# Two recurrences of a layer on TensorE: matmuls of both directions side by side in array halves, outputs ordered by form

## The chip, the cores and the metric

One Trainium2 chip, one of its cores. The metric is the device time of one execution in microseconds: the median of the runs shown. A core has TensorE (PE in the profile, its weight loads PEld), VectorE (DVE), ScalarE (ACT), GpSimd (POOL) and SyncE (SP), which issues most DMAs here. PE writes its products to PSUM, eight banks of 128 partitions by 2 KB.

## The reference, cut to what matters

A layer has 512 latent tokens and 256 context tokens of width 1024. Two mixers run beside each other, each with 8 heads of 128 channels, each in both directions over chunks of 64 tokens: 4 context chunks, then 8 latent chunks. Each head and direction carries a state `S` of 128 by 128 from chunk to chunk.

```
def step(S, xs):                                    # branch A, gated DeltaNet
    u_c, w_c, qd_c, kd_c, qk_c, tot_c = xs
    v_new = u_c - jnp.einsum('bhcd,bhdv->bhcv', w_c, S)
    o_c = jnp.einsum('bhcd,bhdv->bhcv', qd_c, S) + jnp.einsum('bhij,bhjv->bhiv', qk_c, v_new)
    S = tot_c[..., None, None] * S + jnp.einsum('bhcd,bhcv->bhdv', kd_c, v_new)
    return S, o_c
...
def step(S, xs):                                    # branch B, HGRN2
    qd_c, kd_c, v_c, tot_c = xs
    o_c = jnp.einsum('bhcd,bhdv->bhcv', qd_c, S)
    S = tot_c[..., :, None] * S + jnp.einsum('bhcd,bhcv->bhdv', kd_c, v_c)
    return S, o_c
```

The outputs of both directions are added, normed and gated. The branches are merged, and an expert layer of 16384 experts follows, which takes about the second half of the time and is not touched here.

## The kernel before, in words

The program is a list of Python generators whose steps are interleaved in proportions (`weave`, `mixed`). From that list the framework that builds the program places each engine's instructions in a fixed order before the run; an instruction may be placed ahead of others that come earlier in the list but aren't ready by the framework's reckoning. It also sets all waits. Two accesses of one PSUM tile that lie in the same bank are put in order, whatever parts of the bank they touch, unless both are on the same engine.

PSUM is split in three pools: three banks `a` (`bank`), two banks `s` (`quad`, four blocks of 128 columns) and three banks `pj` for projections.

*Branch A* (lines 469 to 759). For each head `h`, `scan(h)` runs beside `prepare(h + 1)` (keys, queries, values by projection, the inverse of a triangular matrix in `levels`), beside `ada_rows`, and beside `fill`, projections that later stages need. A projection (`proj`) is a run of matmuls of 512 or 256 columns in three parts (lines 99 to 101) over weights split by ScalarE (line 94) and VectorE (line 95).

`scan(h)` has 12 steps, 4 over context and 8 over latents. In step `i` the first direction is at chunk `i`, the second at the last but `i`, so that the two always lie in different halves of the 128 partitions (`blk` gives block, half and half's number; `slot` gives the place of a step's pair in the tiles `TB`, `vn` and `edS`, in which the upper half is stored in reverse). One step:

- for each direction, the product of keys and state (line 714, "KS") into its half of block 0 of a `quad`, then a VectorE step on 64 partitions that adds the values (line 715, tile `tmp`); in the first step ScalarE copies the values instead (line 712);
- one matmul with the inverse `TB` for both directions (line 717) into block 1;
- VectorE scales it to `vd` (line 720), and over latents ScalarE copies it to `vn` (line 722);
- for each direction, the product of keys and `vd` (line 726, "K") into block 2 or 3, then a VectorE step that makes the new state (line 732 or 734).

A step takes a `quad` of its own. After the last, the outputs of both directions are made in one `quad` (lines 742 to 747): for each chunk and direction `qd` by state (line 745), then `qk` by `vn` (line 746). `finish` norms and gates them, with another `quad`.

*Branch B* (lines 763 to 913). For each head, `scan_b(h)` runs beside `prepare_b(h + 1)` and `fill`. It has 11 steps; in each, for each direction, one matmul (line 883, K again) into a quarter of a `quad`, which two steps share, then a copy or a VectorE step that makes the new state (line 892). The outputs (lines 899 and 903) use a `bank`.

KS and line 745 use 128 rows by 64 columns of the array, line 746 uses 64 by 64, lines 726 and 883 use 64 by 128, `TB` and the projections all of it. The profile writes these forms as `128*64` and so on.

Of the kernel before, what the change touches and what calls it, by code (L numbers as in the profile page):

```python
# [9 lines left out]
F32 = mybir.dt.float32  # L10
# [50 lines left out]
def program(nc, tc, A, out, dbg=None):  # L61
# [14 lines left out]
    def bc(ap, n):  # L76
        """[p, a] -> [p, a, n]"""
        return ap[:, :, None].to_broadcast([ap.shape[0], ap.shape[1], n])

    def bm(ap, n):  # L80
        """[p, a] -> [p, n, a]"""
        return ap[:, None, :].to_broadcast([ap.shape[0], n, ap.shape[1]])
# [137 lines left out]
    def proj(g, ctx):  # L220
        """128 channels on partitions: [128, 512 latents], [128, 256 context]"""
# [10 lines left out]
    def mixed(*gens):  # L232
        """the steps of several generators in turn, in proportion to the numbers given; a third item marks
        one that need not end here"""
        g = [[x[0], 0, x[1], True, len(x) > 2] for x in gens]
        while any(x[3] and not x[4] for x in g):
            x = min((x for x in g if x[3]), key=lambda x: (x[1] + 1) / x[2])
            x[1] += 1
            x[3] = next(x[0], x) is not x
            yield  # L240
# [69 lines left out]
    def nat(ap):  # L310
        """scan-ordered latents read in natural order"""
        return ap.rearrange("p (c r) -> p r c", r=8)

# [8 lines left out]
    def turned(t, p, steps, b0, n, x):  # L322
        """the upper half of the partitions with directions and blocks in reverse: [p, d, b, x]"""
# [5 lines left out]
    def slot(i, ctx):  # L329
        """a step's place: the chunks of both directions lie in different halves of the partitions"""  # L330
# [108 lines left out]
    def ada_rows():  # L439
        """the rest of the adaLN projection as rows: g1, shift 2, scale 2, g2"""  # L440
# [28 lines left out]
    with tc.tile_pool(name="pA", bufs=1) as pA:  # L469
        # natural order with a zero before, between and after latents and context  # L470
# [10 lines left out]
        def diag(t, z):  # L481
            """the block of a half of the partitions"""
# [7 lines left out]
        def head(t, h):  # L490
            """[p, b, (d h)] -> [p, d, b] of a head"""
# [5 lines left out]
        def conv(dst, ci, ctx):  # L497
# [15 lines left out]
            S.activation(dst, cv[:, :w], AF.Silu)  # L513
# [24 lines left out]
        def prepare(h):  # L538
# [4 lines left out]
            # decays of both directions  # L543
# [11 lines left out]
            # gram matrices, [chunk row, chunk column]  # L555
# [7 lines left out]
            V.scalar_tensor_tensor(br[:, 2], head(eg, h), -1.0, rnk, op0=OP.mult, op1=OP.mult)  # L563
            qk = pA.tile([128, 2, 4, 64], F32, name="qk", bufs=2)
            G.tensor_tensor(qk, E_[:, :, :4], m_in2[:, :, None, :].to_broadcast([128, 2, 4, 64]), op=OP.mult)
            # minus the strict part's entries (the masks come later)
            G.tensor_tensor(E_, E_, br[:, 1, :, :, None].to_broadcast([128, 2, 6, 64]), op=OP.mult)
            V.tensor_tensor(E_, E_, gl_[:, None].to_broadcast([128, 2, 6, 64]), op=OP.mult)
            # diagonal blocks of 16 inverted with a block on each partition
# [49 lines left out]
            yield from conv(vT, 16 + h, True)  # L619
# [10 lines left out]
            H[h] = (kt, qn, rnq, br, qk, ktm, vtm, GA[h])  # L630
            yield

        def ahead(h):
            """the gate of a head and the keys of the next"""
# [54 lines left out]
        def scan(h):  # L689
            kt, qn, rnq, br, qk, ktm, vtm, ga = H[h]  # L690
# [7 lines left out]
            prev = [None, None]  # L698
            for st in range(12):
# [4 lines left out]
                q4 = quad()  # L704
                tmp = pA.tile([128, 128], F32, name="tmp", bufs=3)
                C = []
                for d in range(2):
# [3 lines left out]
                    if prev[d] is None:  # L711
                        S.copy(tmp[s], vtm[s, b])
                    else:
                        T.matmul(q4[s, 0], ksl(kt, c, ctx), prev[d], start=True, stop=True)
                        V.scalar_tensor_tensor(tmp[s], q4[s, 0], br[s, 2, d, b:b + 1], vtm[s, b],
                                               op0=OP.mult, op1=OP.add)
                T.matmul(q4[:, 1], TB[:, sd, sb], tmp, start=True, stop=True)
                if more:
                    vd = pA.tile([128, 128], F32, name="vd", bufs=3)
                    V.tensor_scalar(vd, q4[:, 1], edS[:, sd, sb, h:h + 1], None, op0=OP.mult)  # L720
                if not ctx:
                    S.copy(vn[:, sd, sb], q4[:, 1])
                for d, (b, s, hf) in enumerate(C):
                    lt = order[d][1]
                    if more:
                        T.matmul(q4[:, 2 + d], ktm[s, b], vd[s], start=True, stop=True)
                        if ctx and i < 3:
                            nxt = pA.tile([128, 128], F32, name="sc_", bufs=3)
                        else:
                            nxt = Sx[d][:, lt[0] if ctx else lt[i + 1]]  # L730
                        if prev[d] is None:
                            V.tensor_copy(nxt, q4[:, 2 + d])
                        else:
                            V.scalar_tensor_tensor(nxt, prev[d], etot[:, hf, b, 8 * d + h:8 * d + h + 1],
                                                   q4[:, 2 + d], op0=OP.mult, op1=OP.add)
# [4 lines left out]
            # outputs of both directions  # L740
            po = quad()
            for c in range(8):
                b, s, _ = blk(c, False)
                for d in range(2):
                    T.matmul(po[s, b], qd[:, d, 64 * c:64 * c + 64], Sx[d][:, c], start=(d == 0), stop=False)
                    T.matmul(po[s, b], qk[s, d, b], vn[(s, *slot(7 - c if d else c, False))],
                             start=False, stop=(d == 1))
# [15 lines left out]
    with tc.tile_pool(name="pB", bufs=1) as pB:  # L763
# [15 lines left out]
        # keys whose half of a chunk lies outside the causal range of the queries' half are zero here  # L779
# [15 lines left out]
        def prepare_b(h):  # L795
# [15 lines left out]
            def pick(o, step, n, rep):  # L811
                """one element of each chunk: [p, d, chunk, repeated]"""
# [39 lines left out]
        def scan_b(h):  # L852
            vt, kdt, et, E1, E2, E3 = K[h]
            # scores of pairs of chunks, [keys, queries]: the masks clear the blocks of two different chunks
# [18 lines left out]
            for st in range(11):  # L873
                ctx = st < 4
                i = st if ctx else st - 4
                for d in range(2):
                    lt = order[d][1]
                    c = order[d][0][i] if ctx else lt[i]
                    b, s, _ = blk(c, ctx)
                    if st % 2 == 0 and d == 0:  # L880
                        q4 = quad()
                    pu = q4[:, 2 * (st % 2) + d]
                    T.matmul(pu, kdt[s, 6 * d + b], vt[s, b], start=True, stop=True)
# [4 lines left out]
                    if prev[d] is None:  # L888
                        S.copy(nxt, pu)
                    else:  # L890
                        j = (8 if ctx else 0) + c
                        V.scalar_tensor_tensor(nxt, prev[d], et[:, d, j:j + 1], pu, op0=OP.mult, op1=OP.add)
                    prev[d] = nxt
                yield
# [166 lines left out]
    with tc.tile_pool(name="pE", bufs=1) as pE, tc.tile_pool(name="ps4", bufs=1, space=PSUM) as ps4:  # L1061
# [48 lines left out]
        with tc.tile_pool(name="pR", bufs=1, side="right") as pR:  # L1110
# [30 lines left out]
            def routing(b):  # L1141
# [22 lines left out]
                # rows a and columns b of the candidates: starts of the rows are 16a, 8a + 8, 4a + 24 or a + 48  # L1164
# [243 lines left out]
```

## Time and profile before

| | us |
|---|---|
| runs | 3085.27, 3078.58, 3072.75 |
| median | 3078.58 |
| profiled execution: span from first to last instruction | 3060.6 |
| median less this span | 18.0 |

No whole time is given for the profiled execution beside its span; the span stands for it, and 18.0 us is what lies around it if that execution was like the median.

How to read the rows: a row of a group of instructions has line, engine, operation, out<-in by the program's names, the form of the array (for PE) and the shapes, the count, then busy time in us and the mean ns of one, and behind the next bar the idle time of the engine before them and what ended it. In a timeline the columns are start and duration in us, and equal neighbours are merged, with their count behind the x. Matmuls are pipelined, so their durations overlap: the time that one takes on PE is read from its start to the start of the next. A float32 matmul stands as two instructions, so that one matmul is x2.

### The profile page before, as it was taken

How to read it: one execution, taken by the hardware profiler on the slowest of the kernel's cores; microseconds unless marked ns; L12 is line 12 of the kernel's file. 1: busy time of each engine (PE TensorE's matmuls, PEld its weight loads, DVE VectorE, ACT ScalarE, POOL GpSimd, SP SyncE). 2: the span in 40 equal slices, each digit the busy share in tenths (PEclk: the TensorE clock that was granted, in tenths of full speed). 3: DMA queues.
4: the chain of work that ended last, by engine and by line, in shares of the span. 5: the costliest groups of instructions: out<-in, count | busy, mean ns of one | idle time of the engine just before them, and what ended most of it. 6: DMA issues, size and time to landing. Idle time of an engine off the chain costs nothing.

```text
span 3060.6 us, 40793 instructions
## 1 busy us (share of the span) xinstructions
PE 2875.4 (94%) x15664; PEld 2277.6 (74%) x15664; DVE 1848.8 (60%) x3273; ACT 1122.3 (37%) x1647; POOL 1100.0 (36%) x674
## 2 busy tenths in 40 slices
PE   6899999999999999999999799999999999999998
PEld 3777667766776666667788678787888888887776
DVE  6555455455453567734578957455577766666668
ACT  3433323333332555515223244434333333333333
POOL 2313223232220222200003625252466655655665
PEclk9999999999999989999999788898899999999999
DMA  5323223232232323326423656564788888878885
GB/s 204 98 67 90 67 70 95 75 86 77 83 83 68 112 81 104 100 89 204 158 92 109 199 184 207 185 212 155 252 289 283 294 279 273 291 280 286 285 279 195
DMA packets 243732, 507.92 MB, mean 166 GB/s; under 512 B 56736, under 2 KB 125760, under 8 KB 239440
## 3 DMA queue, kind: packets, MB, share of 16 engines
q1 hardware_dynamic: 206672, 371.07, 37.5%
q0 software_dynamic: 36864, 134.23, 12.4%
q8 instruction: 123, 2.02, 0.3%
q14 instruction: 73, 0.60, 0.1%
HBM read 440.37 MB, written 64.86 MB: 165 GB/s over the span
## 4 chain that ended last, share of the span: by engine, by line
PE 34%; DMA 10%; DVE 6%; issue 2%; ACT 2%; POOL 1%; SPq 0%; ACTq 0%; DVEq 0%; POOLq 0%
DMA wraw<-in_u_t 6%; PE pS L101 4%; PE pS L99 4%; PE pS L100 4%; PE oacc L100 3%; DMA wraw<-in_v_rows 3%; PE oacc L101 3%; PE oacc L99 3%; DVE wlo L95 2%; ACT whi L94 1%; PE pq L99 1%; PE pq L101 1%; PE pq L100 1%; DVE gscr L1098 1%; PE psc L1132 0%
## 5 line engine op out<-in xcount | busy, mean ns | idle before, releaser
L94 ACT CAST whi<-wraw 128x1024 fp32r<-128x1024 f32 x384 | 402.9, 1050 | 893.3 <-DMA wraw<-in_v_rows 225.8
L95 DVE TENSOR_TENSOR wlo<-wraw,whi 128x1024 fp32r<-128x1024 f32 x333 | 491.1, 1475 | 328.0 <-ACT whi L94 321.9
L99 PE MATMUL pS<-tTh,whi 128*128 128x384 f32 x1024 | 377.8, 369 | 36.1 <-ACT whi L94 24.3
L101 PE MATMUL pS<-tTh,wlo 128*128 128x384 f32 x1024 | 374.6, 366 | 10.7 <-POOL wlo L95 6.6
L100 PE MATMUL pS<-tTl,whi 128*128 128x384 f32 x1024 | 373.5, 365 | 0.0
L99 PE MATMUL oacc<-whi,ah 128*128 128x512 f32 x768 | 302.8, 394 | 16.1 <-ACT ah L1281 16.1
L100 PE MATMUL oacc<-wlo,ah 128*128 128x512 f32 x768 | 304.2, 396 | 2.7 <-DVE wlo L95 2.6
L101 PE MATMUL oacc<-whi,al 128*128 128x512 f32 x768 | 303.6, 395 | 0.9 <-DVE al L1282 0.9
L99 PE MATMUL pcl<-hTh,whi 128*128 128x512 f32 x704 | 301.1, 428 | 0.0
L1277 POOL TENSOR_TENSOR ag<-af,gread 128x384 f32<-128x384 f32 x128 | 224.4, 1753 | 211.8 <-DVE al L1282 201.1
L101 PE MATMUL pcl<-hTh,wlo 128*128 128x512 f32 x704 | 292.0, 415 | 0.0
L100 PE MATMUL pcl<-hTl,whi 128*128 128x512 f32 x704 | 290.9, 413 | 0.0
L99 PEld LDWEIGHTS pS<-tTh,whi 128*128 128x128 f32 x1024 | 215.4, 210 | 45.6 <-ACT whi L94 27.2
L95 POOL TENSOR_TENSOR wlo<-wraw,whi 128x1024 fp32r<-128x1024 f32 x51 | 125.8, 2469 | 313.5 <-ACT whi L94 219.8
L1095 POOL DMA_INDIRECT gr<-in_u_rows,eidx x128 | 178.7, 1396 | 142.9 <-DVE gscr L1098 101.2
L101 PEld LDWEIGHTS pS<-tTh,wlo 128*128 128x128 f32 x1024 | 214.4, 209 | 16.2 <-POOL wlo L95 7.9
L100 PEld LDWEIGHTS pS<-tTl,whi 128*128 128x128 f32 x1024 | 214.3, 209 | 3.3
L1095 POOL DMA_INDIRECT gr<-in_v_rows,eidx x128 | 191.6, 1497 | 67.1 <-DVE gacc L1102 46.9
L99 PEld LDWEIGHTS oacc<-whi,ah 128*128 128x128 f32 x768 | 146.2, 190 | 47.6 <-ACT ah L1281 18.8
L100 PEld LDWEIGHTS oacc<-wlo,ah 128*128 128x128 f32 x768 | 146.1, 190 | 35.1 <-DVE wlo L95 5.7
L101 PEld LDWEIGHTS oacc<-whi,al 128*128 128x128 f32 x768 | 145.9, 190 | 33.2 <-DVE al L1282 2.9
L1098 DVE SCALAR_TENSOR_TENSOR gscr<-gr,ttk 128x1024 bf16<-128x1024 f32 x128 | 169.5, 1324 | 0.7
(1197 smaller groups left out, 5462.5 us busy)
## 6 DMA issues: line engine op xcount, KB each, us to landing
wraw<-in_u_t SPq DMA_DIRECT2D x128, 512.0 KB, 4.4
wraw<-in_v_rows SPq DMA_DIRECT2D x128, 512.0 KB, 4.7
wraw<-in_w_c SPq DMA_DIRECT2D x88, 512.0 KB, 3.7
GD<-gst SPq DMA_DIRECT2D x24, 1024.0 KB, 4.2
gread<-GD SPq DMA_DIRECT2D x16, 1536.0 KB, 12.9
bw<-in_w_ada SPq DMA_DIRECT2D x64, 256.0 KB, 2.9
afD<-afx SPq DMA_DIRECT2D x56, 192.0 KB, 3.6
af<-afD SPq DMA_DIRECT2D x56, 192.0 KB, 4.7
```

The costliest lines, as they stand in the source:

```text
L94: S.copy(hi, raw)
L95: (eng or V).tensor_tensor(lo, raw, hi.bitcast(F32), op=OP.subtract)
L99: T.matmul(o, Lh, Rh, start=first, stop=False)
L100: T.matmul(o, Lh, Rl, start=False, stop=False)
L101: T.matmul(o, Ll, Rh, start=False, stop=last)
L1095: G.indirect_dma_start(out=r, out_offset=None, in_=A["u_rows" if i < NSEL else "v_rows"], in_offset=IndirectOffsetOnAxis(ap=eidx[:, n:n + ...
L1098: x = V.scalar_tensor_tensor(scr, r, 1.0, ttk, op0=OP.mult, op1=OP.mult, accum_out=gs[:, n:n + 1])
L1277: G.tensor_tensor(ag.rearrange("p (g t) -> p g t", t=GT), af.rearrange("p (g t) -> p g t", t=GT), gr[:, :, e % EG, :], op=OP.mult)
```

## The change

- In branch A's scan, two `quad`s are taken for the whole scan. Both KS of a step go into block 0 of one (`here`), one VectorE step on 128 partitions makes `tmp` for both directions, and in the first step the values are read where they lie. The two K go to block 2 of `here` and block 3 of the other, and the VectorE steps follow both.
- For that, `brS` holds the scales in the order of `slot` (three small copies a head), and the values are stored in that order already by the Silu of their convolution, in four parts (`turn=True`).
- A's outputs: first all 16 products of `qd` and state, then all 16 of `qk` and `vn`, halves in turn.
- Branch B's scan: the matmuls of 4, 4 and 3 steps stand together, each half's in its own `quad`, then the steps that make the states.

Beside this only comments are removed.

```
-        def conv(dst, ci, ctx):
+        def conv(dst, ci, ctx, turn=False):
...
-            S.activation(dst, cv[:, :w], AF.Silu)
+            if turn:
+
+                for o, n in ((0, 4), (NL + 1, 2)):
+                    S.activation(at(dst, o, (128, n), (1, 64)), at(cv, o, (128, n), (1, 64)), AF.Silu)
+                    S.activation(at(dst, o + 64, (128, n), (1, 64)),
+                                 at(cv, o + 128 * n - 64, (-128, n), (1, 64)), AF.Silu)
+            else:
+                S.activation(dst, cv[:, :w], AF.Silu)
...
+            brS = pA.tile([128, 2, 6], F32, name="brS", bufs=2)
+            V.tensor_copy(brS[0:64], br[0:64, 2])
+            for b0, n in ((0, 4), (4, 2)):
+                V.tensor_copy(brS[64:128, :, b0:b0 + n, None], turned(br[:, 2], 64, (6, 1, 0), b0, n, 1))
...
+            pair = [quad(), quad()]
             for st in range(12):
...
-                q4 = quad()
-                tmp = pA.tile([128, 128], F32, name="tmp", bufs=3)
+
+                here, other = pair[st % 2], pair[1 - st % 2]
                 C = []
                 for d in range(2):
                     c = order[d][0 if ctx else 1][i]
                     b, s, hf = blk(c, ctx)
                     C.append((b, s, hf))
-                    if prev[d] is None:
-                        S.copy(tmp[s], vtm[s, b])
-                    else:
-                        T.matmul(q4[s, 0], ksl(kt, c, ctx), prev[d], start=True, stop=True)
-                        V.scalar_tensor_tensor(tmp[s], q4[s, 0], br[s, 2, d, b:b + 1], vtm[s, b],
-                                               op0=OP.mult, op1=OP.add)
-                T.matmul(q4[:, 1], TB[:, sd, sb], tmp, start=True, stop=True)
+                    if prev[d] is not None:
+                        T.matmul(here[s, 0], ksl(kt, c, ctx), prev[d], start=True, stop=True)
+                if prev[0] is None:
+                    tmp = vtm[:, sb]
+                else:
+                    tmp = pA.tile([128, 128], F32, name="tmp", bufs=3)
+                    V.scalar_tensor_tensor(tmp, here[:, 0], brS[:, sd, sb:sb + 1], vtm[:, sb],
+                                           op0=OP.mult, op1=OP.add)
+                T.matmul(here[:, 1], TB[:, sd, sb], tmp, start=True, stop=True)
                 if more:
                     vd = pA.tile([128, 128], F32, name="vd", bufs=3)
-                    V.tensor_scalar(vd, q4[:, 1], edS[:, sd, sb, h:h + 1], None, op0=OP.mult)
+                    V.tensor_scalar(vd, here[:, 1], edS[:, sd, sb, h:h + 1], None, op0=OP.mult)
                 if not ctx:
-                    S.copy(vn[:, sd, sb], q4[:, 1])
-                for d, (b, s, hf) in enumerate(C):
-                    lt = order[d][1]
-                    if more:
-                        T.matmul(q4[:, 2 + d], ktm[s, b], vd[s], start=True, stop=True)
+                    S.copy(vn[:, sd, sb], here[:, 1])
+                if more:
+                    po_ = [here[:, 2], other[:, 3]]
+                    for d, (b, s, hf) in enumerate(C):
+                        T.matmul(po_[d], ktm[s, b], vd[s], start=True, stop=True)
+                    for d, (b, s, hf) in enumerate(C):
+                        lt = order[d][1]
...
                             V.scalar_tensor_tensor(nxt, prev[d], etot[:, hf, b, 8 * d + h:8 * d + h + 1],
-                                                   q4[:, 2 + d], op0=OP.mult, op1=OP.add)
+                                                   po_[d], op0=OP.mult, op1=OP.add)
                         prev[d] = nxt
...
             po = quad()
-            for c in range(8):
+
+            turns = [(2 * b + z, d) for b in range(4) for d in range(2) for z in range(2)]
+            for c, d in turns:
                 b, s, _ = blk(c, False)
-                for d in range(2):
-                    T.matmul(po[s, b], qd[:, d, 64 * c:64 * c + 64], Sx[d][:, c], start=(d == 0), stop=False)
-                    T.matmul(po[s, b], qk[s, d, b], vn[(s, *slot(7 - c if d else c, False))],
-                             start=False, stop=(d == 1))
+                T.matmul(po[s, b], qd[:, d, 64 * c:64 * c + 64], Sx[d][:, c], start=(c < 2 and d == 0), stop=False,
+                         skip_group_check=True)
+            for c, d in turns:
+                b, s, _ = blk(c, False)
+                T.matmul(po[s, b], qk[s, d, b], vn[(s, *slot(7 - c if d else c, False))],
+                         start=False, stop=(c > 5 and d == 1), skip_group_check=True)
...
-            for st in range(11):
-                ctx = st < 4
-                i = st if ctx else st - 4
-                for d in range(2):
+
+            for s0, s1 in ((0, 4), (4, 8), (8, 11)):
+                pu = [quad(), quad()]
+                cs = []
+                for st in range(s0, s1):
+                    ctx = st < 4
+                    for d in range(2):
+                        c = order[d][0][st] if ctx else order[d][1][st - 4]
+                        b, s, hf = blk(c, ctx)
+                        cs.append((st, d, c, ctx, hf))
+                        T.matmul(pu[hf][:, st - s0], kdt[s, 6 * d + b], vt[s, b], start=True, stop=True)
+                yield
+                for st, d, c, ctx, hf in cs:
+                    i = st if ctx else st - 4
                     lt = order[d][1]
...
-                        S.copy(nxt, pu)
+                        S.copy(nxt, pu[hf][:, st - s0])
...
-                        V.scalar_tensor_tensor(nxt, prev[d], et[:, d, j:j + 1], pu, op0=OP.mult, op1=OP.add)
+                        V.scalar_tensor_tensor(nxt, prev[d], et[:, d, j:j + 1], pu[hf][:, st - s0],
+                                               op0=OP.mult, op1=OP.add)
                     prev[d] = nxt
-                yield
+                    if d:
+                        yield
```

## Rows read from the trace of the kernel before

**Rows 1.** The page: its first line, and the busy time of each engine.

```profile
span 3060.6 us, 40793 instructions
...
PE 2875.4 (94%) x15664; PEld 2277.6 (74%) x15664; DVE 1848.8 (60%) x3273; ACT 1122.3 (37%) x1647; POOL 1100.0 (36%) x674
```

**Rows 2.** Busy time by stretch: the eight scans of branch A, those of branch B, and some 35 us in the middle of B. Columns: stretch, its length, busy us and instructions of each engine, granted clock, DMA share, GB/s.

```profile
161.00:1016.00 855.00, 827.31 (x5724) 588.44 (x5721) 416.24 (x913) 281.99 (x499) 201.20 (x126) 0.99 0.27 78
1080.00:1356.00 276.00, 266.02 (x1423) 183.93 (x1423) 173.29 (x257) 128.78 (x225) 62.06 (x33) 0.97 0.27 89
...
1216.00:1251.00 35.00, 33.96 (x188) 23.43 (x188) 25.37 (x38) 19.63 (x34) 9.88 (x6) 1.00 0.30 102
```

**Rows 3.** Groups of PE instructions in B's stretch (1080 to 1356 us): the matmuls of the recurrence.

```profile
L883 PE MATMUL quad<-vt_b,kdt 64*128 64x128 f32 x334 | 75.7, 326 | 3.5 <-DVE Sx_b L892 2.0 <-DVE sd__8910 L892 1.5
```

**Rows 4.** Who waited for whom in A's stretch: the longest of PE's matmuls, and the copy vn. Columns: waiting instruction, what ended the wait, us in all, times, longest.

```profile
PE quad L726 <- DVE vd L720: 11.4, 6, 3.5
...
ACT vn L722 <- DVE vd L720: 96.7, 36, 7.6
```

**Rows 5.** PE in order of time in A: a lone KS (L714) among projections, and a K (L726) directly ahead of a KS.

```profile
450.09 0.39 PE L101 MATMUL pcl<-hTh,wlo 128*128 128x512 f32 x1
450.41 0.43 PE L714 MATMUL quad<-Sx,kt 128*64 128x128 f32 x2
450.77 0.50 PE L99 MATMUL pcl<-hTh,whi 128*128 128x512 f32 x1
451.11 0.39 PE L100 MATMUL pcl<-hTl,whi 128*128 128x512 f32 x1
451.34 0.40 PE L101 MATMUL pcl<-hTh,wlo 128*128 128x512 f32 x1
...
472.16 0.49 PE L726 MATMUL quad<-vd,ktm 64*128 64x128 f32 x2
472.58 0.43 PE L714 MATMUL quad<-Sx,kt 128*64 128x128 f32 x2
```

**Rows 6.** PE in order of time in the outputs of A.

```profile
360.08 0.43 PE L745 MATMUL quad<-Sx,qd 128*64 128x128 f32 x2
360.44 0.43 PE L746 MATMUL quad<-vn,qk 64*64 64x128 f32 x2
360.80 0.43 PE L745 MATMUL quad<-Sx,qd 128*64 128x128 f32 x2
```

**Rows 7.** PE in order of time in B: two K (x4), four products of one form (L903 x8), and a lone K among projections.

```profile
1080.50 0.49 PE L883 MATMUL quad<-vt_b,kdt 64*128 64x128 f32 x4
1080.92 0.39 PE L101 MATMUL pcx<-hTh,wlo 128*128 128x256 f32 x1
...
1097.07 0.66 PE L903 MATMUL po<-Sx_b,E 128*64 128x128 f32 x8
1097.66 0.49 PE L899 MATMUL po<-vt_b,sc_b 128*128 128x128 f32 x2
...
1123.46 0.40 PE L99 MATMUL pcl<-hTh,whi 128*128 128x512 f32 x1
1123.79 0.49 PE L883 MATMUL quad<-vt_b,kdt 64*128 64x128 f32 x2
1124.20 0.51 PE L100 MATMUL pcl<-hTl,whi 128*128 128x512 f32 x1
```

**Rows 8.** Groups of VectorE and ScalarE instructions in A's stretch.

```profile
L715 DVE SCALAR_TENSOR_TENSOR tmp<-quad,br,vtm 64x128 f32<-64x128 f32 x176 | 61.5, 350 | 100.8 <-PE quad L714 98.8
L734 DVE SCALAR_TENSOR_TENSOR Sx<-Sx,etot,quad 128x128 f32<-128x128 f32 x112 | 38.8, 346 | 83.3 <-PE quad L726 83.1
L563 DVE SCALAR_TENSOR_TENSOR br<-eg,rn 128x12 f32<-128x12 f32 x7 | 1.1, 164 | 0.0
...
L423 ACT ACTIVATE sp<-pcx 128x256 f32<-128x256 f32 x17 | 6.4, 377 | 1.7 <-PE pcx L101 1.6
L513 ACT ACTIVATE vT<-cv 128x769 f32<-128x769 f32 x7 | 5.9, 844 | 6.5 <-DVE cv L508 6.5
```

**Rows 9.** All engines in order of time in A: from a K to the new state, and from KS to K.

```profile
461.19 0.49 PE L726 MATMUL quad<-vd,ktm 64*128 64x128 f32 x2
461.72 0.35 DVE L734 SCALAR_TENSOR_TENSOR Sx<-Sx,etot,quad 128x128 f32<-128x128 f32 x1 [0.41 <-PE quad L726]
...
466.02 0.43 PE L714 MATMUL quad<-Sx,kt 128*64 128x128 f32 x2
466.49 0.34 DVE L715 SCALAR_TENSOR_TENSOR tmp<-quad,br,vtm 64x128 f32<-64x128 f32 x1 [0.20 <-PE quad L714]
...
468.23 0.38 PE L717 MATMUL quad<-tmp,TB 128*128 128x128 f32 x2
468.65 0.35 DVE L720 TENSOR_SCALAR vd<-quad,edS 128x128 f32<-128x128 f32 x1 [0.66 <-PE quad L717]
469.72 0.26 ACT L722 COPY vn<-quad 128x128 f32<-128x128 f32 x1
470.10 0.49 PE L726 MATMUL quad<-vd,ktm 64*128 64x128 f32 x2
```

More of the change, by code (lines that the diff above doesn't have):

```diff
@@ L618, in prepare @@
             vT = pA.tile([128, WG], F32, name="vT")
-            yield from conv(vT, 16 + h, True)
+            yield from conv(vT, 16 + h, True, turn=True)
             ktm = pA.tile([128, 6, 128], F32, name="ktm", bufs=2)
@@ L629, in prepare @@
             yield from mixed((levels(h, E_, XD, br), 10), (ahead(h), 14))
-            H[h] = (kt, qn, rnq, br, qk, ktm, vtm, GA[h])
+            H[h] = (kt, qn, rnq, brS, qk, ktm, vtm, GA[h])
             yield
@@ L689, in scan @@
         def scan(h):
-            kt, qn, rnq, br, qk, ktm, vtm, ga = H[h]
+            kt, qn, rnq, brS, qk, ktm, vtm, ga = H[h]
             qd = pA.tile([128, 2, NL], F32, name="qd")
@@ L710, in scan @@
                     C.append((b, s, hf))
-                    if prev[d] is None:
-                        S.copy(tmp[s], vtm[s, b])
-                    else:
-                        T.matmul(q4[s, 0], ksl(kt, c, ctx), prev[d], start=True, stop=True)
-                        V.scalar_tensor_tensor(tmp[s], q4[s, 0], br[s, 2, d, b:b + 1], vtm[s, b],
-                                               op0=OP.mult, op1=OP.add)
-                T.matmul(q4[:, 1], TB[:, sd, sb], tmp, start=True, stop=True)
+                    if prev[d] is not None:
[7 more added lines that the diff above has]
+                T.matmul(here[:, 1], TB[:, sd, sb], tmp, start=True, stop=True)
                 if more:
                     vd = pA.tile([128, 128], F32, name="vd", bufs=3)
-                    V.tensor_scalar(vd, q4[:, 1], edS[:, sd, sb, h:h + 1], None, op0=OP.mult)
+                    V.tensor_scalar(vd, here[:, 1], edS[:, sd, sb, h:h + 1], None, op0=OP.mult)
                 if not ctx:
-                    S.copy(vn[:, sd, sb], q4[:, 1])
-                for d, (b, s, hf) in enumerate(C):
-                    lt = order[d][1]
-                    if more:
-                        T.matmul(q4[:, 2 + d], ktm[s, b], vd[s], start=True, stop=True)
+                    S.copy(vn[:, sd, sb], here[:, 1])
[5 more added lines that the diff above has]
+                        lt = order[d][1]
                         if ctx and i < 3:
-                            nxt = pA.tile([128, 128], F32, name="sc_", bufs=3)
+                            nxt = pA.tile([128, 128], F32, name="sc_", bufs=4)
                         else:
@@ L731, in scan @@
                         if prev[d] is None:
-                            V.tensor_copy(nxt, q4[:, 2 + d])
+                            V.tensor_copy(nxt, po_[d])
                         else:
                             V.scalar_tensor_tensor(nxt, prev[d], etot[:, hf, b, 8 * d + h:8 * d + h + 1],
-                                                   q4[:, 2 + d], op0=OP.mult, op1=OP.add)
+                                                   po_[d], op0=OP.mult, op1=OP.add)
                         prev[d] = nxt
@@ L872, in scan_b @@
             prev = [None, None]
-            for st in range(11):
-                ctx = st < 4
-                i = st if ctx else st - 4
-                for d in range(2):
-                    lt = order[d][1]
[L878 to L883, printed above, removed]
+            for s0, s1 in ((0, 4), (4, 8), (8, 11)):
[11 more added lines that the diff above has]
+                    i = st if ctx else st - 4
+                    lt = order[d][1]
                     if ctx and i < 3:
```

## The prediction

> **What bounds the kernel now.** I read the page's busy line first: PE is busy 94% of a span of 3060.6 us, VectorE 60%, ScalarE and POOL 37 and 36% [rows 1]. The change touches two stages only, so the next view is the busy time by stretch [rows 2]. Branch A's eight scans run from 161 to 1016 us: PE is busy 827 of 855 us, VectorE 416, ScalarE 282. Branch B's run from 1080 to 1356 us: PE 266 of 276, VectorE 173, and in the middle of it 35 us are about one head, of which PE works 34 and VectorE 25. TensorE is the bound of both, and what else happens beside it is hidden as long as PE always has something to do. The view of waits agrees: the longest wait of a PE instruction in A in sum is 11.4 us, before L726 [rows 4].
>
> A busy PE need not stream columns, so the third view is the order of time on PE, read by start to start. Each float32 matmul stands there as two records (x2), because it runs in two passes. A projection matmul of 512 columns follows the last at 0.23 us (451.11 to 451.34). With one state product L714 (128 rows by 64 columns of the array, hence "KS") before it, everything around it gets longer: the L101 ahead of it takes 0.32 instead of 0.23, L714 itself 0.36, and the L99 behind it 0.34 instead of 0.23 [rows 5]. One lone KS matmul so costs 0.09 + 0.36 + 0.11 = 0.56 us. For the update product L726 ("K", 64 rows by 128 columns) the like-formed L883 shows it: 0.33 for the L99 ahead, 0.41 itself, and again 0.11 behind, 0.62 us in all [rows 5, 7]. A good half of this isn't arithmetic but the change from one form of the array to another. In the outputs every matmul changes form: L745, L746, L745 in 0.72 us, 0.36 each [rows 6].
>
> What like-formed neighbours in the two halves of the array cost is in the trace too. Four records of L883, two matmuls, take 0.42 us (1080.50 to 1080.92), as against 0.41 for one; eight records of L903, four matmuls, take 0.59 us (1097.07 to 1097.66) [rows 7]. So two matmuls in different halves take as long as one (0.01 more), and each further pair adds 0.59 - 0.37 = 0.22 us: two passes of 0.11.
>
> **The change part by part.** *Scan of A, 11 steps a head with KS and K, 88 in all.* Before, the second direction's KS waits for the first one's VectorE step, since both use one PSUM bank, and other matmuls come between: the waits between accesses of one bank are seen where ScalarE's copy vn waits for VectorE's vd though both only read [rows 4]. After, both KS stand in the program with nothing between, and K of the two directions go to two banks. A KS pair then saves 0.56 - 0.01 = 0.55 us, a K pair 0.62 - 0.01 = 0.61, together 1.16 x 88 = 102 us. Not all of it is there: a K often stands directly ahead of the next KS and shares its switch (472.16 to 472.58) [rows 5], about 0.2 us in half the steps, 9 us; and a neighbour that is itself a small matmul gets less long than a projection. I take 80. A second deduction: the first K writes the bank that vn is read from and must wait for vn; the second K goes to the other bank and need not. In the trace vd starts at 468.65, vn at 469.72, K at 470.10 [rows 9]. In the 7 latent steps of a head the pair may therefore come apart. Bounds: 0 of 56 (80 us saved) and 56 of 56 (80 - 56 x 0.61 = 46). I take half, 63 us.
>
> *Outputs of A.* Now 32 matmuls a head at 0.36 us: 11.5 us, 92 in all. After: 8 pairs with one form, then 8 pairs with the other, each 0.37 + 7 x 0.22 = 1.9 us, 3.8 a head and 30 in all. Saved: 62 us. Bound below: if they only stood by form and did not overlap, 0.11 us a pass, 64 passes are 7.0 us a head and 36 us are saved.
>
> *Edits off PE.* One VectorE step tmp a step goes, 88 x 0.35 = 31 us of VectorE [rows 8]; the chain of a step is shorter by it. Three small copies brS a head come in (nearest row: L563, 0.16 us each [rows 8], under 1 us a head), and the Silu of v is cut from one of 0.84 us into four (nearest row: L423, 0.38 us for 256 columns [rows 8]; at most 0.7 us more a head); two ScalarE copies a head go. VectorE is at half load and ScalarE at a third in A [rows 2], so I cost them at nothing; without that cover they are 8 x 1.5 = 12 us. No DMA is added or moved. Both PSUM tiles of the pool are now held through a whole scan, so the next head's scan still waits for the norm of this head's outputs, as before; cost between 0 and the 3.8 us of the outputs a head; I take 0, as PE has projections then.
>
> *Scan of B.* Now 176 matmuls L883 (334 of 352 records fall in the stretch [rows 3]) of 0.62 us, 109 us; some stand two together, I take 102. After: bursts of 8, 8 and 6 a head. A burst of 8 is 0.42 + 3 x 0.22 + 0.21 for the switch at its ends = 1.29 us, one of 6 is 1.07; 3.65 a head, 29 in all. PE has 73 us less to do, 9 us a head. The price: a burst needs both PSUM tiles, so it waits until the eight VectorE steps of the last burst have read them, 8 x 0.35 = 2.8 us; 16 such waits are 0 to 45 us.
>
> The TensorEngine Tiling page of the Trainium skill warns here (PSUM Bottleneck): packing speeds up TensorE but not the emptying of PSUM. By row, the emptying in B is two VectorE steps a matmul pair of 0.35 us, and VectorE's 25 us a head would be level with PE's 34 - 9 = 25.
>
> *Sum.* On PE: A 63 + 62 = 125 us, B 73. Not all arrives. In A no other engine comes near (VectorE 416 - 31 of some 750 us), but the order on PE is fixed beforehand and shorter matmuls hide less of the others' latency; I keep 85%, 105 us. In B PE and VectorE are then level at 25 us a head, and two engines that wait for each other don't both run full; from 34.5 (276 / 8) I expect 28.8 us, 46 us for eight heads. 151 us in all: the span goes from 3060.6 to 2910. The median of the runs shown lies 18 us above this span, so 2928 us.
>
> One rule speaks against the column halves. The TensorE: Matmul & The Clock Gate page of the Trainium skill (Part 3: Packing small matmuls) says that a weight load overlaps matmuls in flight "only when row_grp differs". KS and the first output form use all rows and differ in columns only. By it their pairs would not overlap: 0.21 us x 88 and 1.6 us x 8 less saved, 31 us. The trace disagrees: L903 is of that very form, and four of it take 0.59 us instead of 4 x 0.21 + 0.2 = 1.04.
>
> **The rivals.** *All of it arrives.* All K pairs stay together and PE stays the bound: 80 + 62 + 73 = 215, 2865 us. For: PE is idle only 28 of 855 us now. Against: vn, and VectorE in B.
> *VectorE and the chains take over.* B falls only to 31 us a head (30 us), A gives 75 since K pairs fall apart and PE waits more: 2974 us. For: VectorE's 25 of 35 us.
> *Lock step is laid open; slower.* Before, the directions were staggered: one's VectorE step ran while the other's matmul did. After, both wait at the same points. One step's chain, by rows 9: KS to tmp 0.47, tmp 0.35, TB to vd 0.42, vd 0.35, vn 0.26, K to S 0.53, two S 0.70: 3.1 us, of which PE itself fills 1.0. If PE's fixed order put nothing between, 2.1 us a step open, 96 steps, 200 us against 125 saved: A +75, B -46, 3108 us. It decides from 1.3 us new idle a step. Against it: projections stand between all dependent matmuls now [rows 5], and 12 such steps are 37 us of the some 94 that a head would take.
> *The change doesn't do what it says*: the builder sets projections between the pairs all the same, or halves don't overlap. Then the outputs alone by form, 36, and little else: around 3040; with splits everywhere and new waits, no change.
>
> **How the numbers follow.** Forecast 0.50 (2895 to 2965), all of it 0.15, VectorE and chains 0.20, not what it says 0.08 (half of it no change), lock step 0.07. The range reaches from just above "all of it" to beyond "VectorE and chains", 2870 to 3010. Runs of before differ by 12.5 us, so 0.5%, 15 us, is what can be told from no change. Faster: 0.50 + 0.15 + 0.20 + 0.03 = 0.88; same 0.05; slower 0.07.
>
> **What would show it.** On PE in order of time: L714's successor as x4 with about 0.37 us to the next start, the K pair as x4 with 0.42 (split in the latent steps if vn matters), the outputs as two blocks of x32 records in 1.9 us each, B's bursts as x16 in about 1.1 us. A's stretch about 750 us, B's head about 29. Wrong would be: x2 records as before, idle time before the step's matmuls of over 1 us a step, or B's heads at 33 us and more.

## The result, and the profile after

The changed kernel takes 2932.0 us (median of four runs, 2928.0 to 2939.3) against 3075.9 before: ratio 0.953, interval 0.950 to 0.957. The forecast was 2928 us. The total is right; its two halves are not. (The list of the change lacks one thing: tile `sc_`, which holds A's states over the context, has four buffers instead of three. No run tests it by itself.)

First the page of the changed kernel: its span and the busy time of each engine, beside [rows 1].

```profile
span 2926.2 us, 40749 instructions
...
PE 2703.8 (92%) x15664; PEld 2225.6 (76%) x15664; DVE 1827.0 (62%) x3209; ACT 1119.5 (38%) x1654; POOL 1117.0 (38%) x674
```

TensorE executes the same 15664 matmul passes and is busy 172 us less; the span is 134 us shorter. (The profiled run took 2928.0 us, 1.8 more than its span.) To see where, I cut both traces at the same landmarks: A from 161 us to the last matmul of its last output, then B from its first product pq (queries by keys, L884 after) to its last output, then the tail, until the merge begins. Busy time by stretch, of the kernel before (B and tail; A is in [rows 2]):

```profile
1054.00:1353.00 299.00, 284.87 (x1539) 199.37 (x1538) 193.25 (x275) 145.45 (x248) 74.40 (x37) 0.97 0.26 88
1353.00:1372.00 19.00, 19.00 (x86) 15.73 (x85) 5.55 (x5) 5.14 (x7) 0.00 (x0) 1.00 0.45 151
```

and of the changed kernel (A, B, tail):

```profile
161.00:887.00 726.00, 686.45 (x5668) 533.71 (x5664) 390.81 (x845) 279.14 (x503) 201.07 (x126) 0.98 0.31 91
920.00:1187.00 267.00, 234.43 (x1499) 186.51 (x1500) 185.54 (x272) 146.53 (x245) 88.51 (x37) 0.90 0.28 93
1187.00:1230.00 43.00, 43.00 (x192) 35.57 (x191) 10.79 (x9) 12.37 (x16) 0.00 (x0) 1.00 0.42 135
```

A ends 129 us earlier (1016 to 887), the merge begins 142 us earlier (1372 to 1230), and the 8 us that are then lost are in the stages behind, which the change doesn't touch. So A gave 129 and everything from A's end to the merge gave 13. The two are not quite the work's own: the projections that fill gaps are taken wherever the builder finds a place, and A holds 56 matmul records fewer than before (5724 to 5668), the tail 106 more at 0.22 us (43.00 / 192). With 56 x 0.23 = 13 us put back, A's own gain is some 116 us and B's 26. The third thing to see is B's granted clock: 0.97 before, 0.90 after.

How little B's heads gained shows where both kernels do the same work: five heads, from the last output product of B's second head to that of its seventh, first before, then after.

```profile
1141.40:1317.10 175.70, 169.79 (x942) 117.05 (x937) 122.33 (x173) 92.87 (x158) 47.76 (x24) 1.00 0.29 96
```

```profile
989.40:1160.30 170.90, 149.28 (x942) 118.62 (x938) 122.70 (x174) 95.81 (x160) 61.81 (x25) 0.88 0.28 93
```

The same 942 records take 170.9 instead of 175.7 us. TensorE is busy 20.5 us less, but idle 21.6 instead of 5.9, and its clock is 0.88 instead of 1.00. The rest of B's 32 us lies in its first two heads and its last, which hold fewer projections than before.

TensorE in order of time in the changed kernel: a KS pair, a K pair that stays together and one that comes apart, the outputs of a head, a burst in B.

```profile
170.70 0.49 PE L740 MATMUL quad<-vd,ktm 64*128 64x128 f32 x4
171.13 0.50 PE L99 MATMUL pcl<-hTh,whi 128*128 128x512 f32 x1
...
174.08 0.32 PE L724 MATMUL quad<-sc__1496,kt 128*64 128x128 f32 x1
174.08 0.32 PE L724 MATMUL quad<-sc__1498,kt 128*64 128x128 f32 x1
174.24 0.27 PE L724 MATMUL quad<-sc__1496,kt 128*64 128x128 f32 x1
174.24 0.27 PE L724 MATMUL quad<-sc__1498,kt 128*64 128x128 f32 x1
174.45 0.50 PE L99 MATMUL pcl<-hTh,whi 128*128 128x512 f32 x1
...
191.40 0.48 PE L740 MATMUL quad<-vd,ktm 64*128 64x128 f32 x2
...
192.64 0.49 PE L740 MATMUL quad<-vd,ktm 64*128 64x128 f32 x2
...
438.40 1.97 PE L762 MATMUL quad<-Sx,qd 128*64 128x128 f32 x32
440.30 1.96 PE L766 MATMUL quad<-vn,qk 64*64 64x128 f32 x32
442.20 0.50 PE L99 MATMUL pcl<-hTh,whi 128*128 128x512 f32 x1
...
1066.78 1.16 PE L903 MATMUL quad<-vt_b,kdt 64*128 64x128 f32 x16
1067.87 0.50 PE L100 MATMUL pcl<-hTl,whi 128*128 128x512 f32 x1
```

The four KS records are two matmuls whose passes begin at the same moments (174.08, 174.24): the halves of the array truly work side by side, 0.37 us for both. All 88 KS pairs stand so, and 74 of 88 K pairs (0.43 us, 170.70 to 171.13). In the other 14 some projections come between (five from 191.40 to 192.64), until vn has been copied. The outputs of a head take 3.80 us (438.40 to 442.20) instead of 32 x 0.36 = 11.5. A whole burst of B takes 1.09 us.

Then the waits of TensorE's matmuls (waiting instruction, what ended the wait, us in all, times, longest), the two longest of A's stretch, then those of B's:

```profile
PE quad L740 <- DVE vd L734: 18.1, 13, 3.4
PE quad L731 <- DVE tmp L729: 11.0, 7, 2.6
...
PE pkb L853 <- POOL kd L842: 22.9, 7, 4.8
PE quad L903 <- DVE Sx_b L916: 6.1, 4, 2.7
```

The longest wait in B isn't in the recurrence. It is that of a head's transposes (L853) for POOL's product kd (L842), which takes 4.4 us (median); before, this wait summed to 1.8 us. The product itself got longer: its median is 3.4 us in the kernel before, 3.4 and 3.5 in the two runs below that keep B's old scan beside a shorter A, and 4.4 here. Why isn't shown. Next the matmuls that end two standstills, with the idle time before them, and a piece of a burst, and behind it the busy time of three stretches around them:

```profile
972.45 0.48 PE L903 MATMUL quad<-vt_b,kdt 64*128 64x128 f32 x2 [2.71 <-DVE Sx_b L916]
975.50 2.39 PE L853 MATMUL pkb<-ident,kd 128*128 128x128 f32 x10 [2.56 <-POOL kd L842]
977.82 1.23 PE L903 MATMUL quad<-vt_b,kdt 64*128 64x128 f32 x8
```

```profile
972.00:975.00 3.00, 0.48 (x2) 0.29 (x2) 3.00 (x4) 2.11 (x2) 3.00 (x1) 0.91 0.19 75
975.00:985.00 10.00, 9.50 (x35) 7.19 (x36) 5.53 (x9) 2.43 (x6) 0.44 (x1) 0.52 0.50 157
985.00:1008.00 23.00, 21.25 (x159) 17.74 (x157) 16.12 (x26) 14.77 (x24) 11.02 (x5) 1.00 0.18 58
```

TensorE stands for 2.71 and then 2.56 us, and the granted clock falls from 1.00 to about 0.5, from 2.4 to 1.2 GHz, for the next 10 us. The piece of a burst that comes in it takes 1.17 us for eight records (977.82 to 978.99), where the whole burst above took 1.09 for sixteen. The whole of B has seven falls, 55 us at the low level, against two falls and 17 us before.

### The profile page after: what moved, and what is told of

The parts are those of the page before. It is cut to its first block, busy times and chain, and to the rows that moved or that the text cites. A ratio compares the mean times of both kernels' runs of the same rounds, so it can differ in the third digit from the quotient of the medians.

```text
span 2926.2 us, 40749 instructions
## 1 busy us (share of the span) xinstructions
PE 2703.8 (92%) x15664; PEld 2225.6 (76%) x15664; DVE 1827.0 (62%) x3209; ACT 1119.5 (38%) x1654; POOL 1117.0 (38%) x674
## 4 chain that ended last, share of the span: by engine, by line
PE 37%; DMA 11%; DVE 6%; issue 2%; ACT 2%; POOL 1%; SPq 0%; ACTq 0%; DVEq 0%; POOLq 0%
DMA wraw<-in_u_t 5%; DMA wraw<-in_v_rows 4%; PE pS L101 4%; PE pS L99 4%; PE pS L100 4%; PE oacc L100 4%; PE oacc L101 4%; PE oacc L99 4%; DVE wlo L95 2%; ACT whi L94 1%; PE pq L99 1%; PE pq L101 1%; PE pq L100 1%; DVE gscr L1124 1%; PE pcl L101 1%
## 5 line engine op out<-in xcount | busy, mean ns | idle before, releaser
L101 PE MATMUL pS<-tTh,wlo 128*128 128x384 f32 x1024 | 374.3, 366 | 11.5 <-POOL wlo L95 6.4
```

The costliest lines, as they stand in the source:

```text
L101: T.matmul(o, Ll, Rh, start=False, stop=last)
```

## The experiments

My theory after this: A's gain is TensorE's own time as predicted; B's is given back by standstills, to which POOL's kd contributes, and by the clock that falls behind each. The rivals: that B's bursts are worth little by themselves, or that A's edit changes something in B. Each ratio below is to runs of the kernel before that were timed beside it, with medians of 3068.9 to 3077.5 us, so a difference of two medians is good to some 9 us; smaller ones are read from the ratios or the stretches.

**A's part alone** (B's scan put back):

```diff
-            for s0, s1 in ((0, 4), (4, 8), (8, 11)):
-                pu = [quad(), quad()]
...
+            for st in range(11):
...
+                for d in range(2):
...
+                    if st % 2 == 0 and d == 0:
+                        q4 = quad()
+                    pu = q4[:, 2 * (st % 2) + d]
```

> Branch A as changed, branch B as before. Theory: A's part alone takes 129 us off (its stretch went from 855 to about 725 us) and B's part is worth only some 12 us, because PE's time in B turned into waits: 2944 us. Rival: B's part is worth the 46 us of the forecast and something later gives them back: about 2978 us.

Measured 3006.7 us, ratio 0.974 (0.967 to 0.981): A arrives (732 us by row), yet the gain is only 69 us. Its four runs lie from 2979.0 to 3021.0 us, at mean granted clocks from 0.941 down to 0.924; the profile is of the slowest. Its A and B, and one of B's matmuls with the idle time before it:

```profile
166.00:898.00 732.00, 687.79 (x5645) 534.87 (x5643) 391.94 (x842) 279.41 (x503) 200.51 (x125) 0.98 0.31 89
930.00:1285.00 355.00, 337.98 (x1531) 237.22 (x1530) 192.76 (x272) 147.88 (x249) 78.40 (x37) 0.80 0.23 74
```

```profile
1086.85 0.63 PE L1363 MATMUL pt_f<-ident,on 128*128 128x128 f32 x4 [3.20 <-DVE on L1360]
```

The very code of B that took 299 us takes 355, at a mean clock of 0.80: some 145 us of it at the low level, in stretches that each follow a standstill of 1.5 to 6.3 us; the last line shows one, behind which the clock stays low for 37 us. Neither theory had that: A's edit alone makes B slower, by 56 us in this execution. One program in one order varies by 42 us from run to run, and the runs with the lower clock are the longer ones.

**B's part alone** (A as before):

```diff
-            for st in range(11):
...
-                        q4 = quad()
...
+            for s0, s1 in ((0, 4), (4, 8), (8, 11)):
+                pu = [quad(), quad()]
```

> Branch A as before, branch B as changed. Theory: 12 us faster than before, 3064 us, with idle PE time in B's stretch of 30 us or more and a lower granted clock there. Rival (46 us from B): 3030 us.

Measured 3045.0, ratio 0.989 (0.985 to 0.993): 31 us, between the two. Its B, to lay beside the 299 us of before:

```profile
1061.00:1323.00 262.00, 230.37 (x1475) 184.80 (x1475) 183.48 (x272) 141.63 (x242) 88.55 (x37) 0.91 0.29 94
```

37 us shorter at the clock of the changed kernel, with 64 matmul records fewer (some 15 us, done elsewhere). So the bursts are worth 31 us alone, and 3006.7 - 2932.0 = 75 us once A is changed.

**The outputs of A alone**, on the kernel before:

```diff
-            for c in range(8):
-                for d in range(2):
-                    T.matmul(po[s, b], qd[...], Sx[d][:, c], ...)
-                    T.matmul(po[s, b], qk[s, d, b], vn[...], ...)
+            turns = [(2 * b + z, d) for b in range(4) for d in range(2) for z in range(2)]
+            for c, d in turns:
+                T.matmul(po[s, b], qd[...], Sx[d][:, c], ...)
+            for c, d in turns:
+                T.matmul(po[s, b], qk[s, d, b], vn[...], ...)
```

> The kernel before with A's outputs ordered by form alone, the recurrences as before. If form order and overlapping halves give 11.5 - 3.8 us a head on a PE that is the bound: 62 us off, 3014 us. If only the changes of form go and the halves don't overlap: 36 us off, 3040 us.

Measured 3073.0, ratio 1.000 (0.998 to 1.003): no gain at all. Its A and B, then three stretches of B, and in a second view a standstill there:

```profile
164.00:963.00 799.00, 771.87 (x5708) 572.96 (x5702) 418.41 (x913) 281.92 (x499) 199.75 (x126) 0.98 0.29 83
999.00:1358.00 359.00, 331.68 (x1534) 235.18 (x1533) 197.05 (x273) 146.90 (x248) 73.38 (x37) 0.81 0.23 73
...
1021.00:1049.00 28.00, 26.64 (x78) 18.91 (x79) 11.41 (x21) 9.87 (x13) 1.47 (x1) 0.51 0.32 106
1049.00:1062.00 13.00, 10.94 (x70) 7.29 (x69) 9.99 (x9) 5.91 (x15) 4.04 (x2) 1.00 0.02 6
1062.00:1100.00 38.00, 36.71 (x118) 27.31 (x118) 15.26 (x25) 12.15 (x16) 5.44 (x4) 0.51 0.18 63
```

```profile
1063.29 1.09 PE L1345 MATMUL pt_f<-ident,on 128*128 128x128 f32 x4 [3.35 <-DVE on L1342]
```

A is 56 us shorter, as the outputs promise, and B 60 us longer, now at 0.81. Behind one standstill of 3.35 us the clock stays low for 38 us here. A saving of 56 us has vanished without a trace in the total; only the stretches show it.

**The outputs and B's bursts together**, on the kernel before (the last two edits in one):

> The kernel before with the ordered outputs in A and the bursts in B, A's recurrence as before. Alone the outputs gave nothing (their 56 us came back in B, where PE stood at its lower clock for 137 us) and B alone 32 us. If the low clock is a matter of B's old order after standstills, the two together give 56 + 32 = 88 us: 2988 us. If the gains just don't add: 3040 us.

Its B:

```profile
1002.00:1267.00 265.00, 235.93 (x1477) 187.11 (x1476) 181.22 (x271) 144.30 (x244) 89.63 (x37) 0.88 0.29 92
```

Measured 2995.4, ratio 0.973 (0.970 to 0.977). The same edit that was worth nothing is worth 50 us (3045.0 to 2995.4) beside the bursts: with these, and nothing else changed in B, it is 262 to 272 us under every A that was run.

**The outputs in their old order**, in the changed kernel (the edit to the outputs turned round):

> The changed kernel with A's outputs in their old order (form changing with every matmul); the recurrences and B stay changed. Theory: with B's bursts in place its clock recovers within 10 us of a standstill, so A's outputs are worth their PE time there, 8 x (11.5 - 3.5) = 64 us: 2996 us. If something else gives the outputs' gain back, as in the run with them alone: 2940 us.

Its A:

```profile
162.00:948.00 786.00, 746.32 (x5654) 553.98 (x5650) 391.72 (x844) 278.56 (x503) 201.08 (x126) 0.98 0.29 83
```

Measured 2992.2, ratio 0.973 (0.970 to 0.977): the outputs give 60 us, all in A (786 to 726).

**Halves not side by side**: outputs by form, first all of the lower half, then all of the upper.

```diff
-turns = [(2 * b + z, d) for b in range(4) for d in range(2) for z in range(2)]
+turns = [(2 * b + z, d) for z in range(2) for b in range(4) for d in range(2)]
```

> The changed kernel, but in A's outputs all products of the lower half stand first, then all of the upper half; the order by form stays. If two halves must stand side by side to run at once, a pass costs 0.107 us alone and the outputs take 7.0 instead of 3.5 us a head: 28 us slower than the changed kernel, 2960 us. If the order by form is all that counts: 2932 us.

Its A by stretch, and the outputs of a head on TensorE:

```profile
164.00:910.00 746.00, 708.15 (x5658) 555.93 (x5653) 388.72 (x845) 279.66 (x503) 200.14 (x126) 0.98 0.31 88
```

```profile
445.40 3.33 PE L762 MATMUL quad<-Sx,qd 128*64 128x128 f32 x32
448.66 3.32 PE L766 MATMUL quad<-vn,qk 64*64 64x128 f32 x32
451.92 0.50 PE L99 MATMUL pcl<-hTh,whi 128*128 128x512 f32 x1
```

Measured 2947.8, ratio 0.958 (0.954 to 0.962). The same 64 passes take 6.52 us a head (445.40 to 451.92) instead of 3.80: eight heads 22 us, and A is 20 us longer. Of the 7.7 us a head that the order gives, 5.0 come from the like forms, 2.7 from the halves side by side. In the total it is 16 us, not the 28 expected, and the intervals of this run and of the changed kernel overlap.

**More fillers for B** (`NFB = 10` to `14`), the cure if B only lacked projections to stand in its gaps:

> The changed kernel with more projections mixed into branch B (NFB 14 instead of 10). Theory: in B, PE waits and so falls to its lower clock because too few projections stand between the dependent steps; the 44 us of projections that are left behind B are moved into its idle time, and B's clock rises from 0.90: 20 to 35 us faster than the changed kernel, about 2905 us. Rival: B's wait is set by its own chain and the static order doesn't let projections in: same, 2932 us.

Its B and its tail:

```profile
924.00:1230.00 306.00, 274.76 (x1687) 222.95 (x1687) 196.23 (x280) 158.06 (x261) 87.88 (x37) 0.89 0.31 100
1230.00:1234.00 4.00, 3.71 (x17) 2.72 (x15) 0.83 (x1) 0.47 (x1) 0.00 (x0) 1.00 0.60 197
```

Measured 2932.7, ratio 0.957 (0.953 to 0.960): no gain. The tail goes from 43 to 4 us, and B is 39 longer. TensorE still idles 31 us of B: the fillers stand elsewhere than in the gaps.

**The same on the kernel before**, to see whether any other order lowers the clock of B's old scan:

> The kernel before, nothing of the change, with more projections mixed into B (NFB 14 instead of 10). If B's old order is close to the lower clock whatever A does, some other order of it shows over 60 us at the lower clock in B and the kernel is 20 to 50 us slower, about 3110 us. If B's old order holds its clock by itself: same, 3077 us.

Its B:

```profile
1056.00:1366.00 310.00, 296.18 (x1542) 208.79 (x1542) 193.09 (x273) 145.76 (x247) 74.37 (x37) 0.93 0.25 85
```

Measured 3075.0, ratio 1.001 (0.999 to 1.003). The clock moves (0.97 to 0.93, 42 us low instead of 17), yet far from 0.80: this doesn't settle why a shorter A costs the old B so much.

**A head further ahead** (`KB = 1` to `2`), so that kd is ready long before its transposes:

> The changed kernel with two buffers for the keys and sums of B's preparation (KB 2 instead of 1), so that the next head's preparation can begin earlier. If that chain over one buffer sets B's 34 us a head: B's 267 us shrink by 20 us or more, 2910 us. If the wait is at POOL's product kd (4.4 us) and VectorE's order whatever the buffers: 2932 us.

Its B by stretch, and two waits of TensorE's matmuls there, the longest and that for kd:

```profile
928.00:1199.00 271.00, 236.05 (x1504) 194.53 (x1504) 179.65 (x273) 149.35 (x251) 84.48 (x37) 0.86 0.28 94
```

```profile
PE pt_f L1368 <- DVE on L1365: 22.9, 6, 6.8
...
PE pkb L853 <- POOL kd L842: 3.6, 1, 3.6
```

Measured 2935.5, ratio 0.959 (0.954 to 0.963): no gain. The wait for kd shrinks from 22.9 to 3.6 us, and one as long as it was, 22.9 us, stands at the transposes of a head's normalized outputs. Idle time in B moved rather than went.

**kd shared by POOL and VectorE:**

```diff
-G.tensor_tensor(kd, kd, kt, op=OP.mult)
+G.tensor_tensor(kd[:, 0], kd[:, 0], kt[:, 0], op=OP.mult)
+V.tensor_tensor(kd[:, 1], kd[:, 1], kt[:, 1], op=OP.mult)
```

> The changed kernel with POOL's product kd (128x1536, 4.4 us a head) cut in two, one half on VectorE. PE stands still 2.6 us before the transposes of kd where the clock falls. If that stop is what drops the clock: B's clock rises from 0.90 to 0.95 or more and B takes 15 to 25 us less, about 2912 us. If VectorE's extra 1.0 us a head weighs more: 2932 us or a little above.

Its B:

```profile
924.00:1176.00 252.00, 226.70 (x1508) 180.88 (x1508) 180.54 (x278) 144.99 (x244) 81.50 (x37) 0.95 0.30 100
```

Measured 2915.6, ratio 0.952 (0.948 to 0.955). B is 15 us shorter, the clock 0.95, 27 us at the low level instead of 55. TensorE's wait for kd is 15.3 us there instead of 22.9; VectorE's half took some 2.2 us, not 1.0. The intervals of this run and of the changed kernel overlap, and by the ratios the gain is 5 us, not 16: it is shown by the stretch, and by the last run, whose B is nearly as short.

**vn behind the state steps**, so that the second K has no reason to go ahead alone:

```diff
-                if not ctx:
-                    S.copy(vn[:, sd, sb], here[:, 1])
                 if more:
...
                         prev[d] = nxt
+                if not ctx:
+                    S.copy(vn[:, sd, sb], here[:, 1])
                 yield
```

> The changed kernel with the copy vn behind the state steps in A. If the 14 of 88 K pairs that came apart did so because the first K waits for vn: 88 of 88 together, 14 x 0.6 = 8 us less on PE in A, about 2924 us. If the copy then holds up the next step in that bank: same or slower, 2932 to 2940 us.

Its A by stretch, and a K pair of a latent step on TensorE:

```profile
162.00:879.00 717.00, 673.22 (x5647) 524.32 (x5648) 392.17 (x844) 277.10 (x503) 198.45 (x125) 0.98 0.32 91
```

```profile
191.60 0.49 PE L738 MATMUL quad<-vd,ktm 64*128 64x128 f32 x4
```

Measured 2925.3, ratio 0.954 (0.951 to 0.958). All 88 K pairs stand together (x4, 191.60), and A is 9 us shorter, though it also holds 21 matmul records fewer (some 5 us); B takes 272 us, 5 longer. In the total, 7 us is less than the interval can tell.

**Both of these:**

> The changed kernel with both edits that helped: kd cut between POOL and VectorE, and vn copied behind the state steps. If they add: 16 + 7 us off the changed kernel, 2909 us. If B's order, which any edit changes, decides: 2915 to 2930 us.

Its A and B:

```profile
164.00:880.00 716.00, 669.69 (x5667) 522.17 (x5662) 392.43 (x845) 277.56 (x503) 199.33 (x126) 0.98 0.32 92
912.00:1166.00 254.00, 228.75 (x1509) 181.79 (x1510) 180.52 (x278) 144.90 (x244) 81.50 (x37) 0.94 0.30 98
```

Measured 2900.2 us, ratio 0.943 (0.940 to 0.945), clear of the changed kernel's interval: 32 us less than the changed kernel, faster than both. Over kd shared alone it is 15 us by the medians and 28 by the ratios, again clear of the interval, so the move of vn is worth something there; A is 12 us shorter (716 us; 728 with kd shared alone). How much of it is the pairs isn't told apart.

## Why the prediction was right, and where only its total was

*KS and K pairs of A: right.* 0.37 and 0.43 us a pair, as forecast. The deduction for vn was right in kind: pairs come apart in latent steps because of it, and moving the copy puts all together. Its size was not: 14 of 56 are apart, not 28, so by the price used 14 x 0.61 = 9 us more were saved.

*Outputs: right.* 1.90 us a block; 56 to 60 us in A, against 62.

*"I keep 85%, 105 us": mis-sized.* Of the 134 us that TensorE then had less to do by these prices (125 + 9), its busy time shows some 128 at equal work (827 to 686, less the 13). Idle time took 12 (28 of 855 us before, 40 of 726 after), not 20; some 116 us arrived at equal work, 129 with the projections that moved out of A.

*"46 us for eight heads" in B: the step that failed.* At the merge 13 us arrived, 26 at equal work. I had named VectorE as what holds TensorE back. It is busy 186 of 267 us, and the wait of the bursts, which I had bounded by 45 us, is 6.1 us. What TensorE was given back became standstills: its idle time in B rose from 14 to 33 us, the largest wait at POOL's kd, which the prediction doesn't mention. Behind them comes the low clock. The five heads of equal work show the sum. The prediction takes 46 us off TensorE there (73 / 8 a head). Of these, 15.7 went into idle time. Some 17 to 21 went into 41 us at the low level: 21 if all work takes twice its time there, 17 by the B of A's part alone, which has 128 us more of it than before and 53 more of busy time (0.41 us each). 4.8 us arrived. Of the 5 to 8 us that are left, an estimate gives 3 to bursts that projections cut in two (13 of 15, at the prediction's 0.21 us for a change of form); the rest stays open. So a head takes 34.2 us instead of 28.8, and "B's heads at 33 us and more" was one of the prediction's own signs of being wrong. That kd is one cause is shown by its sharing (B 15 us shorter); kb2 shows that it isn't the only one.

*What the prediction left out: the clock.* All its sums are at full clock, and in A they may be (0.97 to 0.99 in all runs). In B they are not. The two errors, 24 us too little in A and 33 too much from there to the merge, nearly cancel, and the 8 us lost behind the merge, with a forecast of 2910 for a span of 2926, are covered by the 18 us that I set around the span. Only 1.8 us lies around the span of the changed kernel; the rest comes from the profiled execution of before, which was shorter than all four of its runs. The right total is partly luck: without the bursts, the change would have been worth 69 us.

*The rule on weight loads* (the Trainium skill, TensorE: Matmul & The Clock Gate, Part 3) by which a weight load doesn't overlap matmuls in flight of a half that differs in columns only: the trace disagrees again. L762 is 128 rows by 64 columns, and its 32 passes take 1.90 us with halves in turn, 3.26 with halves apart (445.40 to 448.66). With no overlap, the forecast would have lost 31 us; it lost none.

*The rivals.* "Lock step" fell: all idle time before the step's own matmuls in A is under 35 us, 0.4 us a step, where it decides from 1.3. "All of it arrives" came near in A alone: 116 us at equal work, and 129 with the moved projections, of its 142. "VectorE and the chains" had the size of B's gain (30 us; 26 at equal work) about right and its engine wrong; its 31 us a head wasn't reached.

*Left open.* Why the old scan of B meets more and longer low-clock stretches as soon as A is shorter. In the traces of before, the changed kernel and the two runs with a shorter A and the old scan, a fall in B follows a standstill of TensorE of 1.5 to 6.3 us; with the old scan and a shorter A the clock then stays low for 7 to 38 us, before for 3.4 and 14, in the changed kernel for 3.4 to 10. The length of the standstill alone doesn't decide it: in A of the changed kernel twelve standstills of 1.5 to 3.4 us brought five falls, of 3.4 to 6.8 us. The fixed order of B is another one after any edit ahead of it, but A's part alone varied by 42 us in one order, and no run set the standstills while holding the rest. Whether K pairs need two PSUM banks was not tried.

## What to carry to other kernels

In this kernel the small matmuls cost mostly the change of the array's form and the wait of one half for the other: ordered by form and with the halves in turn, an output matmul cost a third of what it did in the old order (0.12 us for 0.36). Try that order where yours stand among others. Before summing what a busy TensorE saves, look for the stage behind where it will have to wait, at the engine that is slow there (a POOL product of 4.4 us), and price each standstill with the clock behind it. When an edit that must help moves nothing, compare the stretches and their granted clocks before you drop it: it may be worth 50 us beside another edit.

## What the runs showed of the hardware that was not expected

In B's old scan beside a shorter A, four standstills of TensorE, of 2.0 to 3.4 us, were each followed by 34 to 38 us at 1.2 GHz: the same B took 299 us at a mean granted clock of 0.97, and 355 and 359 at 0.80 and 0.81. Matmuls that differ in both rows and columns of the array (L766, 64 by 64) and write one PSUM bank in different partitions ran as fast side by side as those of L762: 32 passes in 1.90 us.
